# A hybrid attention and convolution layer: the norm weights spread by TensorE, the first loads in another order, and the last pair of heads handed to its out-projection inside the core

## The chip, the core and the metric

The kernel runs on one core of one Trainium2 chip. A core has five engines that run side by side, each through its own instruction list, in order: PE (TensorE, matmuls and transposes; PEld is its weight load), DVE (VectorE), ACT (ScalarE), POOL (GpSimd) and SP (SyncE). SP and POOL here only issue DMAs between DRAM and the core's memory; an issue that has to wait holds up the issues behind it in the same list. The metric is the device time of one execution in microseconds. Three runs of the kernel before gave 921.63, 918.69 and 923.97 us.

## The reference, cut to what matters

```python
def reference(x, norm_g, w_in, conv_w, conv_b, conv_ln_g, conv_ln_b, w_out, final_norm_g):
    for layer in range(DEPTH):                      # one layer, x is 1024 x 1024 float32
        h = rmsnorm(x, norm_g[layer])
        proj = jnp.einsum('bsd,de->bse', h, w_in[layer])          # 1024 -> 5632 columns
        q, k, v, a_gate, c_val, c_glu, c_gate = jnp.split(proj, split_idx, axis=-1)
        y_att = attention_branch(q, k, v, a_gate)
        y_conv = conv_branch(c_val, c_glu, c_gate, conv_w[layer], conv_b[layer],
                             conv_ln_g[layer], conv_ln_b[layer])
        y = jnp.concatenate([y_att, y_conv], axis=-1)
        x = x + jnp.einsum('bse,ed->bsd', y, w_out[layer])
    return rmsnorm(x, final_norm_g)
```

`attention_branch` runs 16 query heads of 64 over 4 key heads, in three dilated causal windows (128 by step 1, 512 by 4, 2048 by 16), whose results are mixed by their softmax denominators, times `silu(a_gate)`. `conv_branch` is `val * sigmoid(glu)`, a causal depthwise convolution of 31 taps, a layer norm, `silu`, and times `silu(c_gate)`.

## The kernel before

**Numbers.** TensorE works in float32r, which keeps fewer bits than float32. So each float32 operand is split in a rounded high part and a low part (`split_r`: ACT casts the high part, DVE subtracts), and each product of two operands is three matmuls: high x high, high x low, low x high. For most blocks of w_in the low part is made otherwise (`split_dma`): ACT writes the high part and its negative, and a DMA on POOL's queue that adds on the way (`add_into`) adds the raw weights to the negative.

**Start.** `prepare(half)` loads x in blocks of 128 rows, squares and sums them on ACT, takes 1/root, multiplies by that and by the norm weights (`gbc`, the row norm_g loaded by one DMA into all 128 partitions), transposes each block on TensorE into two banks `xT`, and splits these into `hhi` and `hlo`, the stationary side of every input projection. Before that TensorE makes 45 idle transposes (`idle`) on the identity.

**Input projections.** A block of 128 columns of w_in (`raw`, split in `wh` and `wl`) times both halves of h gives two banks `ps`, 24 matmuls of 512 columns each. h0 to h7 are the GLU and value blocks of the convolution, k, v, q and a those of attention, c0 to c7 the gate of the convolution. `SECTIONS` says which blocks go beside which pair of heads.

**Attention.** `attend(p)` handles heads 2p and 2p+1: scores `sc`, on DVE table and minimum (`near`, `far`: `add_min`), exponentials `e` on ACT, transposes `tp`, sums `on` and `of` with the high and low parts of v side by side in the 128 output rows. So in `comb` the upper 64 rows have to be added to the lower 64. The kernel does it by DMA: SP stores the lower rows to the tile `y`, POOL's adding DMA adds the upper rows, DVE multiplies by the gate (`y<-y,ag`), and SP stores `y` to `y_dram`, for each of the eight pairs. At the end `att_part(tb)` loads `ya`, 128 columns of all eight pairs, splits it and multiplies by `woah` and `woal`, made by `load_wo_att` from eight loads `raw_oa`, of which two can be held at a time (`opsa`, 16 banks of 24 matmuls).

**Convolution.** `convolve(p)` runs the 31 taps on DVE. `layer_norm(half)` loads the sums again (`cc`), normalizes, gates and stores to `yc_dram`. `load_wo` makes `woc`, and `conv_part(tb)` the last product `opsc` and the final norm.

**Order.** Every operation is recorded with a price and is put in order by a planner (`Plan.order`), which plays the engines through, starting what its prices say can start first, with priority by place in the program and by `boost` (`TUNE`). `LIMITS` says how many tiles of a name may be alive. The result is one fixed order on each engine; in the run the engines wait for one another by semaphores.

Of the kernel before, what the change touches and what calls it, by code (L numbers as in the profile page):

```python
# [34 lines left out]
LIMITS = {"x": 5, "raw": 2, "raw_oc": 1, "raw_oa": 2, "wh": 2, "wl": 3, "tab": 2, "e": 7, "pt": 5, "vs": 4, "vc":  # L35
          4, "turn": 2, "score": 2, "hc": 5, "c": 7, "t": 1, "g": 1, "gl": 7, "y": 1, "ag": 4, "cc": 10, "qs": 6,
          "qf": 4, "kdh": 9, "kdl": 6, "yc": 1, "ya": 2, "zc": 8, "za": 3}
# [3 lines left out]
WARM = 45  # L41
TUNE = {"w": 125, "use": 250, "ln": 65, "att": 230, "conv": 85, "wo": 125, "woa": 100, "ap": 170, "wait": 0.2116}
SECTIONS = [("h1 v k0 q0", 0), ("h2 a0 q1", 1), ("h3 a1 q2", 1), ("h4 a2 q3", 1), ("h5 k1 a3 q4", 1),
            ("h6 a4 q5 c0", 1), ("h7 a5 q6 c1 q7", 1), ("a6 a7 c2 c3", 1), ("c4 c5", 1), ("c6 c7", 0)]
# [115 lines left out]
class Plan:  # L160
# [5 lines left out]
    def __init__(self, tc, slots, limits):  # L166
        self.tc, self.nc = tc, tc.nc
        self.slots = slots
        self.limits = limits
        self.ops = []  # L170
        self.moved = []
        self.prio, self.boost = [], 0
        self.ranks = {}
        self.tables = {}
# [11 lines left out]
    def op(self, engine, cost, fn, outs, ins):  # L186
        i = len(self.ops)
        deps, bufs = set(), set()
# [24 lines left out]
        self.prio.append(i - self.boost)  # L213
# [21 lines left out]
    def act(self, out, x, func, bias=None, scale=None, accum=None):  # L235
        nc = self.nc
        kw = {"bias": bias, "scale": scale, "accum_out": accum}
        kw = {k: v for k, v in kw.items() if v is not None}

        if func in (AF.Exp, AF.Tanh, AF.Sqrt):  # L240
            self.tables[len(self.ops)] = func is AF.Sqrt

        def fn():
            if func is AF.Copy and not kw:
                nc.scalar.copy(out.ap(), x.ap())  # L245
            else:
# [3 lines left out]
        self.op("ACT", (0.051 if near else 0.0935) + x.cols / 1200.0 + 0.0935 * ptrs, fn,  # L250
                [out] + ([accum] if accum else []), [x, bias, scale])

# [4 lines left out]
    def stt(self, out, a, s, b, op0, op1):  # L257
        self.op("DVE", 0.0685 + a.cols / 960.0 + (0.061 if isinstance(s, View) else 0.0),
# [13 lines left out]
    def add_min(self, out, a, b, first, least):  # L272
# [3 lines left out]
                [out, least], [a, b, first])  # L276

# [130 lines left out]
    def trace(self):  # L408
# [40 lines left out]
def layer_kernel(tc, x, norm_g, w_in, conv_w, conv_b, ln_g, ln_b, w_out, fin_g, tab, out):  # L449
# [30 lines left out]
    avg = fixed([P, P], "avg", avg_t, True)  # L480
    par = fixed([P, 8 * NPAR], "par", const([P, 8 * NPAR], "par"), False)
# [47 lines left out]
    idle = bank("sc", "idle")  # L529
    pl.mm([(idle[:, 0:P], ident, ident, None, None)] * WARM)  # L530
    gbc = c4([P, D], "gbc")
    rows = c4([P, D], "rows")

    first_w = {2: C_GLU, 3: C_VAL}
    raw, ready = {}, {}

    def prepare(half):
        xs = []
        for j in range(4):
# [7 lines left out]
        rs = []  # L547
        for j in (0, 2):
            st = pl.buf("st", [P, 8], F32, f"xst{half}{j}")
            ms, v, t, r = (st[:, 2 * k:2 * k + 2] for k in range(4))  # L550
            for k in range(2):
                junk = pl.buf("c2", [P, D], BF16, f"junk{half}{j + k}")
                pl.act(junk, xs[j + k], AF.Square, accum=ms[:, k:k + 1])
            pl.ts(v, ms, 1.0 / D, NORM_EPS, ALU.mult, ALU.add)
            rsqrt(r, v, t)
            rs += [r[:, 0:1], r[:, 1:2]]
        for j in range(4):
            tb = 4 * half + j
            xt, o = xs[j], j * P
# [6 lines left out]
            if tb in first_w:  # L566
                ready[first_w[tb]] = split_w(first_w[tb], raw[tb], split_r)

    def parameters():
# [3 lines left out]
        b = bank("sc", "par_ps")  # L573
# [23 lines left out]
    def load_w(col):  # L597
# [3 lines left out]
        w = split_w(col, load_raw(col))  # L601
# [153 lines left out]

    def attend(p):
# [126 lines left out]
        for r0 in (0, 2):  # L883
            whole = turned(f"w{r0}", [(at(2 * r + j), far_e(j, r0 + r, 1)[:, 0:P])
                                      for r in range(2) for j in range(2)], P)
            for r in (r0, r0 + 1):
# [11 lines left out]
                yield 1.0  # L898
        for j in range(2):
# [60 lines left out]

    wo_conv, wo_att = [], [[[None] * 8, [None] * 8] for _ in range(2)]
# [12 lines left out]
    def outproj(name, tb, y_src, z_src, w, cuts=(0, 512, 1024), after=lambda zc: None):  # L974
        y = c4([P, 8, P], f"y{name}{tb}")
# [3 lines left out]
        yh, yl = c4([P, 8, P], f"yh{name}{tb}", F32R), c4([P, 8, P], f"yl{name}{tb}", F32R)  # L979
        split_r(yh, yl, y)  # L980
        for n0, n1 in zip(cuts, cuts[1:]):
            b = bank("mm", f"ops{name}{tb}_{n0}")[:, 0:n1 - n0]
            half, cs = n0 // 512, slice(n0 % 512, n0 % 512 + n1 - n0)
            for f in range(8):
                wh, wl = w[half][0][f][:, cs], w[half][1][f][:, cs]
                pl.mm([(b, yh[:, f, :], wh, f == 0, False),
                       (b, yh[:, f, :], wl, False, False),
                       (b, yl[:, f, :], wh, False, f == 7)])
# [6 lines left out]
    def att_part(tb):  # L995
        rows = slice(tb % 2 * 512 + tb // 2, tb % 2 * 512 + 512, 4)
        z = yield from outproj("a", tb, y_dram, x[rows, :], wo_att)
        pl.store(z_dram[rows, :], z)

    def conv_part(tb):  # L1000
# [13 lines left out]
        z = yield from outproj("c", tb, yc_dram, z_dram[rows, :], wo_conv, cuts, square)  # L1014
# [90 lines left out]
```

## Time and profile before

| | us |
|---|---|
| median of three runs | 921.63 |
| lowest and highest | 918.69 and 923.97 |
| profiled execution | 918.28 |
| span of its instructions | 916.3 |
| PE busy in the span | 868.6 |

The profile is of one execution. A matmul's row gives its start and how long it takes from start to end; matmuls overlap, so that what one costs in a row of them is the distance of two starts. The square brackets behind a row hold how long the engine was idle before it and what released it. The clock in the windows' rows is the granted clock of TensorE as a share of 2.4 GHz; 0.50 is 1.2 GHz.

### The profile page before, as it was taken

The numbers are of one execution on the slowest core, as the hardware profiler recorded it, in microseconds if no ns is written. First come the engines' busy times: TensorE is split into PE (matmuls) and PEld (weight loads), VectorE is DVE, ScalarE is ACT, GpSimd is POOL, SyncE is SP. The second block draws the span as 40 slices with busy tenths as digits, with TensorE's granted clock in tenths as the row PEclk, the third lists the DMA queues.
The fourth block names the chain that finished last, engine by engine and source line by source line (L and its number), as shares of the span: only waits on it lengthen the run. The fifth ranks groups of instructions, "written<-read, shape, count | busy, mean of one in ns | idle before, by whom it ended". The sixth has DMA issues, their size and how long they took to land.

```text
span 916.3 us, 12908 instructions
## 1 busy us (share of the span) xinstructions
PE 868.6 (95%) x4449; PEld 724.4 (79%) x4449; DVE 649.6 (71%) x1490; ACT 591.8 (65%) x1392; POOL 56.5 (6%) x72
## 2 busy tenths in 40 slices
PE   6899999999999999999998999899994899999996
PEld 6888878888888888878887888788783787878886
DVE  4769985699699899589568846984576953644532
ACT  5743679778878789768956875795897623514211
POOL 0010000011000110011001101001001000000000
PEclk7999999999999999999998999999997899999999
DMA  8732317246554664436506726347969785579111
GB/s 270 196 69 68 93 32 155 47 93 148 108 121 90 132 145 95 80 81 142 137 25 161 161 51 157 71 117 157 282 224 255 245 300 193 172 237 280 64 51 46
DMA packets 106870, 127.19 MB, mean 139 GB/s; under 512 B 18068, under 2 KB 79508, under 8 KB 106806
## 3 DMA queue, kind: packets, MB, share of 16 engines
q1 hardware_dynamic: 98470, 96.49, 34.2%
q0 software_dynamic: 8336, 29.89, 18.4%
q8 instruction: 35, 0.57, 0.2%
q14 instruction: 29, 0.24, 0.1%
HBM read 66.40 MB, written 25.36 MB: 100 GB/s over the span
## 4 chain that ended last, share of the span: by engine, by line
PE 58%; DVE 16%; DMA 13%; ACT 8%; issue 3%; SPq 1%; POOL 0%; DVEq 0%; ACTq 0%; POOLq 0%
PE ps L232 34%; PE opsc L232 10%; DMA y<-comb 6%; DVE c L259 3%; DMA raw_oc<-in_w_out 3%; ACT e L247 3%; PE on L232 2%; PE of L232 2%; DVE cc L259 2%; PE sc_1near L232 2%; DVE t L259 2%; ACT pt L245 1%; DMA x<-in_x 1%; PE sc_0near L232 1%; SPq L280 1%
## 5 line engine op out<-in xcount | busy, mean ns | idle before, releaser
L232 PE MATMUL ps<-hhi,wl 128*128 128x512 f32 (+1 forms) x720 | 282.2, 392 | 14.7 <-DMA wl<-raw 14.7
L232 PE MATMUL ps<-hhi,wh 128*128 128x512 f32 (+1 forms) x720 | 290.7, 404 | 1.1 <-ACT wh L245 1.1
L232 PE MATMUL ps<-hlo,wh 128*128 128x512 f32 (+1 forms) x720 | 281.8, 391 | 0.0
L232 PEld LDWEIGHTS ps<-hhi,wl 128*128 128x128 f32 x720 | 137.1, 190 | 45.5 <-DMA wl<-raw 15.1
L232 PEld LDWEIGHTS ps<-hhi,wh 128*128 128x128 f32 x720 | 137.5, 191 | 24.9 <-ACT wh L245 2.1
L232 PEld LDWEIGHTS ps<-hlo,wh 128*128 128x128 f32 x720 | 137.6, 191 | 23.0 <-issue 0.2
L247 ACT ACTIVATE e<-e,near 128x256 f32<-128x256 f32 (+1 forms) x256 | 114.9, 486 | 19.3 <-DVE near L255 15.6
L259 DVE SCALAR_TENSOR_TENSOR c<-hc,taps,c 128x511 f32<-128x511 f32 (+14 forms) x120 | 88.6, 738 | 2.1 <-ACT c L247 1.8
L259 DVE SCALAR_TENSOR_TENSOR c<-t,taps,c 128x511 f32<-128x511 f32 (+14 forms) x120 | 88.7, 739 | 0.1
L259 DVE SCALAR_TENSOR_TENSOR t<-hc,taps,t 128x511 f32<-128x511 f32 (+6 forms) x112 | 82.9, 740 | 0.9 <-ACT t L247 0.8
L232 PE MATMUL opsc<-woc,yhc 128*128 128x512 f32 (+1 forms) x272 | 80.9, 381 | 0.7 <-ACT yhc L245 0.7
L247 ACT ACTIVATE e<-e,far 128x96 f32<-128x96 f32 (+1 forms) x128 | 53.9, 424 | 29.3 <-DVE far L274 28.3
L283 POOL DMA_DIRECT2D wl<-raw x42 | 36.5, 870 | 390.0 <-ACT wl L247 297.4
L232 PEld LDWEIGHTS opsc<-woc,yhc 128*128 128x128 f32 x272 | 50.0, 188 | 11.4 <-ACT yhc L245 1.1
L232 PE MATMUL opsa<-woah,yla 128*128 128x512 f32 x128 | 50.6, 396 | 2.3 <-DVE yla L255 2.3
L232 PE MATMUL opsc<-woc,ylc 128*128 128x512 f32 (+1 forms) x136 | 51.9, 382 | 0.5 <-DVE ylc L255 0.5
L232 PE MATMUL opsa<-woah,yha 128*128 128x512 f32 x128 | 50.5, 395 | 0.0
L232 PE MATMUL opsa<-woal,yha 128*128 128x512 f32 x128 | 50.5, 394 | 0.0
L245 ACT CAST wh<-raw 128x1024 fp32r<-128x1024 f32 x44 | 45.9, 1043 | 0.7 <-DMA raw<-in_w_in 0.6
L247 ACT ACTIVATE fjunk<-zc 128x512 bf16<-128x512 f32 (+1 forms) x17 | 10.3, 606 | 55.5 <-DVE zc L255 55.5
L247 ACT ACTIVATE e<-e,f 128x96 f32<-128x96 f32 (+1 forms) x128 | 45.0, 438 | 0.1
L247 ACT ACTIVATE wl<-raw 128x1024 fp32r<-128x1024 f32 x42 | 44.5, 1061 | 0.0
(160 smaller groups left out, 1476.5 us busy)
## 6 DMA issues: line engine op xcount, KB each, us to landing
raw<-in_w_in SPq DMA_DIRECT2D x44, 512.0 KB, 5.4
wl<-raw POOLq DMA_DIRECT2D x42, 512.0 KB, 5.0
x<-in_x SPq DMA_DIRECT2D x8, 512.0 KB, 11.0
tab<-in_tab SPq DMA_DIRECT2D x8, 512.0 KB, 3.5
c_dram<-c SPq DMA_DIRECT2D x8, 512.0 KB, 3.1
y<-comb SPq DMA_DIRECT2D x16, 256.0 KB, 3.8
y<-comb POOLq DMA_DIRECT2D x16, 256.0 KB, 4.9
y_dram<-y SPq DMA_DIRECT2D x8, 512.0 KB, 5.4
```

The source lines that it names most:

```text
L232: nc.tensor.matmul(out.ap(), a.ap(), b.ap(), start=start, stop=stop)
L245: nc.scalar.copy(out.ap(), x.ap())
L247: nc.scalar.activation(out.ap(), x.ap(), func, **{k: ap_of(v) for k, v in kw.items()})
L259: lambda: self.nc.vector.scalar_tensor_tensor(out.ap(), a.ap(), ap_of(s), b.ap(), op0, op1),
L280: self.op("SP", 0.48, lambda: self.nc.sync.dma_start(out.ap(), ap_of(src)), [out], [src, after])
L283: self.op("POOL", 1.0, lambda: self.nc.gpsimd.dma_start(ap_of(dst), x.ap(), accum_op=ALU.add), [dst], [x, dst])
```

## The change

1. The norm weights are loaded as one row (`gain`); two matmuls with a row of 1/1024 spread them over the partitions into two PSUM banks, and each block of x is multiplied in two halves of 512 columns. The factor 1/1024 is taken back in the norm's constants. The second block's squares are summed on DVE. Ten more idle transposes stand at the front and 22 between the first blocks.
2. The GLU weights of h0 are loaded ahead of the third block of x. Their low part, and that of the value weights, are made behind the first two blocks' splits. Squares of later blocks are held until a named earlier split has been made (`hold`, which only sets the plan's order).
3. The last pair of heads isn't stored: TensorE adds the halves of `comb` with a matrix of ones (`fold`, float32, into the banks `y7_0` and `y7_1`), DVE multiplies by the gate, and ACT and DVE split the result into `ylast`, which `opsa` reads from the core's memory; `ya` holds seven pairs.
4. The low parts of the last two gate blocks (c6, c7) are made by `split_r` rather than by DMA.
5. Both halves of the layer norm stand with the attention's out-projection; the planner's prices, limits, boosts and the order of blocks are other numbers.

```diff
-LIMITS = {"x": 5, "raw": 2, "raw_oc": 1, "raw_oa": 2, "wh": 2, ... "tab": 2, ... "pt": 5, ... "y": 1, ... "cc": 10, ...
+LIMITS = {"x": 5, "raw": 2, "raw_oc": 1, "raw_oa": 2, "wh": 3, ... "tab": 1, ... "pt": 4, ... "y": 2, ... "cc": 5, ...
-WARM = 45
+WARM = 55
+LATE = C_CG + 6 * P
+MORE = (10, 12)
-TUNE = {"w": 125, "use": 250, "ln": 65, "att": 230, "conv": 85, "wo": 125, "woa": 100, "ap": 170, ...}
+TUNE = {"w": 225, "use": 260, "ln": 65, "att": 240, "conv": -15, "wo": 185, "woa": 20, "ap": 0, ...}
-SECTIONS = [("h1 v k0 q0", 0), ("h2 a0 q1", 1), ...
+SECTIONS = [("k0 q0 h1 v", 0), ("h2 a0 q1", 1), ...
...
-        self.op("ACT", (0.051 if near else 0.0935) + x.cols / 1200.0 + 0.0935 * ptrs, fn,
+        slow = 2.0 if not near and x.cols > 1 and x.idx.ravel()[1] - x.idx.ravel()[0] > 1 else 1.0
+        self.op("ACT", (0.051 if near else 0.0935) + slow * x.cols / 1200.0 + 0.0935 * ptrs + self.cross(out, x), fn,
...
-                self.dma_time[i] = 4.0 * self.moved[i] / (360e3 if e == "SP" else 150e3)
+                self.dma_time[i] = 4.0 * self.moved[i] / (300e3 if e == "SP" else 175e3)
...
-    gbc = c4([P, D], "gbc")
+    gain = c4([1, D], "gain")
+    gbc = [bank("sc", f"gbc{i}") for i in range(2)]
-    first_w = {2: C_GLU, 3: C_VAL}
+    first_w = {1: C_GLU, 3: C_VAL}
...
             if tb == 1:
-                pl.load(gbc, norm_g.partition_broadcast(P))
+                pl.load(gain, norm_g.rearrange("(o d) -> o d", o=1))
...
+            for i in range(2):
+                pl.mm([(gbc[i], avg[0:1], gain[:, i * 512:i * 512 + 512], True, True)])
...
-            pl.stt(xt, xt, rs[j], gbc, ALU.mult, ALU.mult)
             for cg in range(2):
-                b = bank("tp", f"xT{half}{j}_{cg}")
+                part = xt[:, cg * 512:cg * 512 + 512]
+                pl.stt(part, part, r[:, j % 2:j % 2 + 1], gbc[cg], ALU.mult, ALU.mult)
+                b = bank("mm" if tb == 1 else "tp", f"xT{half}{j}_{cg}")
...
+            if tb < len(MORE):
+                pl.mm([(idle[:, 0:P], ident, ident, None, None)] * MORE[tb])
...
-        w = split_w(col, load_raw(col))
+        w = split_w(col, load_raw(col), split_r if col >= LATE else split_dma)
...
+        if p == NH // 2 - 1:
+            for n in range(2):
+                both = bank("tp", f"y{p}_{n}", "turn")
+                pl.mm([(both, fold[:, DH - j * DH:192 - j * DH], comb[:, j, 2 * n:2 * n + 2].flat(), j == 0, j == 1) for j in range(2)])
+                part = y[:, 2 * n:2 * n + 2].flat()
+                pl.stt(part, both, 0.5, ag[p][:, 2 * n:2 * n + 2].flat(), ALU.mult, ALU.mult)
+                split_r(y_last[0][:, 2 * n:2 * n + 2].flat(), y_last[1][:, 2 * n:2 * n + 2].flat(), part)
+            return
...
-        pl.load(z, z_src)
-        pl.load(y, y_src[:, :, tb * P:(tb + 1) * P], after=z)
+        if not last:
+            pl.load(z, z_src)
+        pl.load(y, y_src[:, 0:n, tb * P:(tb + 1) * P], after=w[1][1][7] if last else z)
...
-    section(9, 8.0, [boosted("ln", layer_norm(0))], [(8.0, [boosted("woa", load_wo_att())])])
+    section(9, 8.0, [boosted("woa", load_wo_att())])
-    together((14.0, [boosted("ln", layer_norm(1))]), (8.0, [boosted("wo", load_wo("c", D, wo_conv))]),
+    together((28.0, [boosted("ln", layer_norm(half)) for half in range(2)]), (8.0, [boosted("wo", load_wo("c", D, wo_conv))]),
```

How the instructions stand, at three places. First PE, the front of its list before (xT_0_180 and xT_1_185 are the first block of x, the next two pairs the second and third block):

```order
L230 MATMUL idle<-ident 128x128 x45
L230 MATMUL xT_0_180<-ident,x_145 128x128 x4
L230 MATMUL xT_1_185<-ident,x_145 128x128 x4
L230 MATMUL xT_0_206<-ident,x_147 128x128 x4
L230 MATMUL xT_1_216<-ident,x_147 128x128 x4
L230 MATMUL xT_0_238<-ident,x_151 128x128 x4
L230 MATMUL xT_1_244<-ident,x_151 128x128 x4
L232 MATMUL ps_0_252<-hhi_194,wh_192 128x256
```

And now, with the two matmuls that spread the norm weights:

```order
L234 MATMUL idle<-ident 128x128 x55
L236 MATMUL gbc_182<-gain,avg 128x512
L236 MATMUL gbc_185<-gain,avg 128x512
L234 MATMUL idle<-ident 128x128 x10
L234 MATMUL xT_0_206<-ident,x_158 128x128 x4
L234 MATMUL xT_1_215<-ident,x_158 128x128 x4
L234 MATMUL idle<-ident 128x128 x12
L234 MATMUL xT_0_242<-ident,x_160 128x128 x4
L234 MATMUL xT_1_248<-ident,x_160 128x128 x4
L236 MATMUL ps_0_275<-hhi_234,wh_188 128x256
```

The first projection moved ahead of the third block's transposes; the norm weights' matmuls stand ahead of the first block's.

Next POOL, the end of its list before (y_6842 is the last pair of heads, wl_6864 the low part of the weights of c7):

```order
L283 DMA y_6228<-comb_5915 64x1024 x2
L283 DMA wl_6419<-raw_6265 128x1024
L283 DMA y_6842<-comb_6533 64x1024 x2
L283 DMA wl_6864<-raw_6580 128x1024
L1101 UNCONDITIONAL_BRANCH
```

And now (y_6211 is the last but one pair, wl_6238 and wl_6250 belong to c4 and c5):

```order
L297 DMA y_6211<-comb_5881 64x1024 x2
L297 DMA wl_6238<-raw_6077 128x1024
L297 DMA wl_6250<-raw_6209 128x1024
L1155 UNCONDITIONAL_BRANCH
```

The last pair's adds are gone, and no low part stands behind them.

Last SP, around the loads of the attention's out-projection weights before:

```order
L286 DMA y_6842<-comb_6533 64x1024 x2
L286 DMA g_dram<-g_6827 128x1024
L280 DMA raw_oa_6858<-in_w_out 128x1024
L280 DMA raw_oa_6869<-in_w_out 128x1024
L280 DMA raw_oa_6890<-in_w_out 128x1024
L286 DMA y_dram<-y_6842 128x1024
L286 DMA yc_dram<-cc_0_6287 128x512
L280 DMA raw_oa_6915<-in_w_out 128x1024
L286 DMA yc_dram<-cc_0_6287 128x512
L286 DMA yc_dram<-cc_1_6336 128x512 x2
L280 DMA ya_6949<-y_dram 128x8x128
```

And now (g_6855 is the gate of c6, cc_0_6909 the layer norm's second half):

```order
L294 DMA raw_oa_6720<-in_w_out 128x1024
L294 DMA raw_oa_6722<-in_w_out 128x1024
L294 DMA gl_0_6769<-g_dram 128x2x512
L294 DMA gl_2_6800<-g_dram 128x2x512
L294 DMA gl_4_6833<-g_dram 128x2x512
L294 DMA raw_oa_6883<-in_w_out 128x1024
L300 DMA g_dram<-g_6855 128x1024
L294 DMA raw_oa_6899<-in_w_out 128x1024
L294 DMA cc_0_6909<-c_dram 128x2x512
L294 DMA raw_oa_6913<-in_w_out 128x1024
L294 DMA ya_6981<-y_dram 128x7x128
```

The last weight load no longer stands behind the store of the last pair, but three of the eight still stand in a row of single issues, each of which needs a free one of two tiles.

## Rows read from the trace of the kernel before

**Rows 1.** Windows: us, busy of each engine, PEclk, DMA share, GB/s
```profile
0.00:42.00 42.00, 31.33 (x208) 29.56 (x209) 23.88 (x48) 24.79 (x52) 1.83 (x8) 0.84 0.82 254
42.00:684.00 642.00, 630.92 (x3314) 527.38 (x3314) 500.93 (x1232) 479.69 (x1201) 52.13 (x61) 0.99 0.49 114
684.00:725.00 41.00, 25.55 (x126) 20.80 (x123) 33.98 (x54) 30.20 (x43) 2.52 (x3) 0.79 0.89 265
725.00:819.00 94.00, 91.20 (x400) 73.39 (x398) 53.32 (x84) 34.33 (x48) 0.00 (x0) 1.00 0.67 224
```

**Rows 2.** Waits of PE: us in total, times, longest
```profile
PE ps L232 <- DMA wl<-raw: 14.7, 1, 14.7
PE xT L230 <- DVE hlo L255: 7.8, 3, 3.6
...
PE sc_0far L232 <- ACT qf L245: 1.8, 3, 0.9
```

**Rows 3.** Timeline of the start: start us, us, engine, what [idle before]
```profile
1.46 7.49 PE L230 MATMUL idle<-ident 128*128 128x128 f32 x45 [1.46 <-POOL ident masks.py:199]
...
9.00 2.48 DVE L259 SCALAR_TENSOR_TENSOR x<-x,xst,gbc 128x1024 f32<-128x1024 f32 x2 [1.27 <-DMA gbc<-in_norm_g]
...
10.34 1.09 PE L230 MATMUL xT<-ident,x 128*128 128x128 f32 x8 [1.40 <-DVE x L259]
...
20.13 0.56 PE L232 MATMUL ps<-hhi,wh 128*128 128x256 f32 x1
...
23.37 1.06 ACT L247 ACTIVATE junk<-x 128x1024 bf16<-128x1024 f32 x1 [4.66 <-DMA x<-in_x]
...
25.77 1.33 PE L230 MATMUL xT<-ident,x 128*128 128x128 f32 x8 [2.73 <-DVE hlo L255]
```

**Rows 4.** A window of 2 us in the start
```profile
18.00:20.00 2.00, 1.49 (x7) 1.49 (x8) 2.00 (x3) 0.71 (x2) 0.00 (x0) 0.50 0.21 60
```

**Rows 5.** Timeline from the last pair's sums to the out-projection
```profile
692.61 0.88 PE L232 MATMUL of<-pt,vc 96*128 96x256 f32 x6
...
694.92 1.07 PE L232 MATMUL mean<-csum,avg 128*128 128x512 f32 x2
...
696.11 3.26 SPq L280 DMA_DIRECT2D raw_oa<-in_w_out  x3
...
700.54 0.90 POOL L283 DMA_DIRECT2D wl<-raw  x1
704.78 1.04 ACT L245 CAST woah<-raw_oa 128x1024 fp32r<-128x1024 f32 x1 [3.35 <-DMA raw_oa<-in_w_out]
...
709.74 1.23 DVE L259 SCALAR_TENSOR_TENSOR y<-y,ag 128x1024 f32<-128x1024 f32 x1 [2.06 <-DMA y<-comb]
...
712.17 0.80 PE L232 MATMUL ps<-hhi,wl 128*128 128x512 f32 x1 [14.68 <-DMA wl<-raw]
...
712.77 0.63 PE L232 MATMUL ps<-hhi,wh 128*128 128x512 f32 x1
```

**Rows 6.** Groups by shape on DVE: xcount, busy us, mean ns, idle before
```profile
L255 DVE TENSOR_TENSOR comb<-of,comb 128x512 f32<-128x512 f32 x32 | 22.0, 687 | 7.4 <-PE of L232 7.2
...
L255 DVE TENSOR_TENSOR woal<-raw_oa,woah 128x1024 fp32r<-128x1024 f32 x8 | 9.8, 1220 | 3.3 <-ACT woah L245 3.3
```

**Rows 7.** The tile raw_oa: its loads from issue to landing
```profile
DMA to landing us min/median/max: 3.2/6.2/9.9
```

**Rows 8.** The tile opsa: durations ns, first and last start
```profile
L232 PE MATMUL opsa<-woah,yha x128: 387/393/477, 724.7 to 817.7; 128*128 128x512 f32 x128
```

**Rows 9.** Groups by shape on ACT, two casts of 512 columns
```profile
L245 ACT CAST qf<-qs 128x512 fp32r<-128x512 f32 x32 | 34.3, 1120 | 13.0 <-DVE qs L259 12.8
...
L245 ACT CAST hhi<-xT 128x512 fp32r<-128x512 f32 x16 | 8.9, 584 | 5.1 <-PE xT L230 5.1
```

**Rows 10.** Waits of DVE for the adding DMAs
```profile
DVE y L259 <- DMA y<-comb: 10.3, 7, 2.3
```

**Rows 11.** A window of 4 us behind a wait in the middle
```profile
496.00:500.00 4.00, 3.82 (x16) 3.58 (x17) 3.92 (x15) 3.67 (x16) 0.00 (x0) 0.50 0.98 213
```

More of the change, by code (lines that the diff above doesn't have):

```diff
@@ L170, in __init__ @@
         self.ops = []
+        self.hold = []
         self.moved = []
@@ L187, in op @@
         i = len(self.ops)
+        ins, self.hold = list(ins) + self.hold, []
         deps, bufs = set(), set()
@@ L257, in stt @@
     def stt(self, out, a, s, b, op0, op1):
-        self.op("DVE", 0.0685 + a.cols / 960.0 + (0.061 if isinstance(s, View) else 0.0),
+        self.op("DVE", 0.0685 + a.cols / 960.0 + (0.061 if isinstance(s, View) else 0.0) + self.cross(out, a),
                 lambda: self.nc.vector.scalar_tensor_tensor(out.ap(), a.ap(), ap_of(s), b.ap(), op0, op1),
@@ L276, in add_min, with square_sum @@
                 [out, least], [a, b, first])
+    def square_sum(self, out, a, total):
+        self.op("DVE", 0.07 + a.cols / 960.0,
+                lambda: self.nc.vector.tensor_tensor_reduce(out.ap(), a.ap(), a.ap(), 1.0, 0.0, ALU.mult, ALU.add,
+                                                            total.ap()), [out, total], [a])
     def load(self, out, src, after=None):
@@ L543, in prepare @@
             if tb == 1:
-                pl.load(gbc, norm_g.partition_broadcast(P))
+                pl.load(gain, norm_g.rearrange("(o d) -> o d", o=1))
             if tb in first_w:
                 raw[tb] = load_raw(first_w[tb])
[L547 to L556, printed above, removed]
+        if half == 0:
+            for i in range(2):
+                pl.mm([(gbc[i], avg[0:1], gain[:, i * 512:i * 512 + 512], True, True)])
         for j in range(4):
             tb = 4 * half + j
+            if j % 2 == 0:
+                st = pl.buf("st", [P, 8], F32, f"xst{half}{j}")
+                ms, v, t, r = (st[:, 2 * k:2 * k + 2] for k in range(4))
+                for k in range(2):
+                    junk = pl.buf("c2", [P, D], BF16, f"junk{half}{j + k}")
+                    if k and j == 0 and half == 0:
+                        pl.square_sum(junk, xs[j + k], ms[:, k:k + 1])
+                    else:
+                        if half:
+                            pl.hold = [hhi[0][:, 4:8, (j + 1) * P:(j + 2) * P]]
+                        elif k:
+                            pl.hold = [hhi[0][:, 4:8, 0:P]]
+                        pl.act(junk, xs[j + k], AF.Square, accum=ms[:, k:k + 1])
+                pl.ts(v, ms, 1.0 / D / D ** 2, NORM_EPS / D ** 2, ALU.mult, ALU.add)
+                rsqrt(r, v, t)
             xt, o = xs[j], j * P
-            pl.stt(xt, xt, rs[j], gbc, ALU.mult, ALU.mult)
             for cg in range(2):
-                b = bank("tp", f"xT{half}{j}_{cg}")
+                part = xt[:, cg * 512:cg * 512 + 512]
+                pl.stt(part, part, r[:, j % 2:j % 2 + 1], gbc[cg], ALU.mult, ALU.mult)
+                b = bank("mm" if tb == 1 else "tp", f"xT{half}{j}_{cg}")
                 pl.mm([(b[:, i * P:(i + 1) * P], xt[:, (4 * cg + i) * P:(4 * cg + i + 1) * P], ident, None, None)
@@ L565, in prepare @@
                 split_r(hhi[half][:, 4 * cg:4 * cg + 4, o:o + P], hlo[half][:, 4 * cg:4 * cg + 4, o:o + P], b.split(P))
-            if tb in first_w:
-                ready[first_w[tb]] = split_w(first_w[tb], raw[tb], split_r)
+            if tb < len(MORE):
+                pl.mm([(idle[:, 0:P], ident, ident, None, None)] * MORE[tb])
+            for k in sorted(first_w) if tb == 1 else ():
+                col = first_w[k]
+                w = c4([P, ND, P], f"wh{col}", F32R), c4([P, ND, P], f"wl{col}", F32R)
+                pl.act(w[0], raw[k], AF.Copy)
+                pl.hold = [hlo[0][:, 0:4, P:2 * P]]
+                pl.tt(w[1], raw[k], w[0].cast(F32), ALU.subtract)
+                ready[col] = w
     def parameters():
@@ L753, in convolve @@
             pl.add_into(csum, c.flat())
+    y_last = [c4([P, 4, 256], f"ylast{k}_", F32R) for k in range(2)]
     def attend(p):
@@ L959, in load_wo @@
             yield 1.0
+    pl.tt(fold[:, DH:P], ident[:, 0:DH], ident[:, DH:P], ALU.add)
     wo_conv, wo_att = [], [[[None] * 8, [None] * 8] for _ in range(2)]
@@ L972, in load_wo_att, with outproj @@
             yield 1.0
-    def outproj(name, tb, y_src, z_src, w, cuts=(0, 512, 1024), after=lambda zc: None):
-        y = c4([P, 8, P], f"y{name}{tb}")
+    def outproj(name, tb, y_src, z_src, w, last=(), cuts=(0, 512, 1024), after=lambda zc: None):
+        n = 8 - len(last)
+        y = c4([P, n, P], f"y{name}{tb}")
         z = c4([P, D], f"z{name}{tb}")
-        pl.load(z, z_src)
-        pl.load(y, y_src[:, :, tb * P:(tb + 1) * P], after=z)
-        yh, yl = c4([P, 8, P], f"yh{name}{tb}", F32R), c4([P, 8, P], f"yl{name}{tb}", F32R)
+        if not last:
+            pl.load(z, z_src)
+        pl.load(y, y_src[:, 0:n, tb * P:(tb + 1) * P], after=w[1][1][7] if last else z)
+        yh, yl = c4([P, n, P], f"yh{name}{tb}", F32R), c4([P, n, P], f"yl{name}{tb}", F32R)
         split_r(yh, yl, y)
+        if last:
+            pl.load(z, z_src, after=yl)
+        rows = [(yh[:, f, :], yl[:, f, :]) for f in range(n)] + list(last)
         for n0, n1 in zip(cuts, cuts[1:]):
-            b = bank("mm", f"ops{name}{tb}_{n0}")[:, 0:n1 - n0]
+            b = bank("mm", f"ops{name}{tb}_{n0}", "opsa" if name == "a" else None)[:, 0:n1 - n0]
             half, cs = n0 // 512, slice(n0 % 512, n0 % 512 + n1 - n0)
@@ L996, in att_part @@
         rows = slice(tb % 2 * 512 + tb // 2, tb % 2 * 512 + 512, 4)
-        z = yield from outproj("a", tb, y_dram, x[rows, :], wo_att)
+        z = yield from outproj("a", tb, y_dram, x[rows, :], wo_att,
+                                [tuple(v[:, tb // 2, tb % 2 * P:tb % 2 * P + P] for v in y_last)])
         pl.store(z_dram[rows, :], z)
@@ L1013, in conv_part @@
         rows = slice((tb % 4) * 256 + tb // 4, (tb % 4) * 256 + 256, 2)
-        z = yield from outproj("c", tb, yc_dram, z_dram[rows, :], wo_conv, cuts, square)
+        z = yield from outproj("c", tb, yc_dram, z_dram[rows, :], wo_conv, (), cuts, square)
         st = pl.buf("st", [P, 8], F32, f"fst{tb}")
```

28 lines of the change are left out of this document (17 added, 11 removed).

## The prediction

> **What bounds the kernel.** I read the windows by stage first [rows 1]. The reader is to see that TensorE is the engine without slack: busy 630.9 of 642 us in the projections and attention, 91.2 of 94 in the out-projection of attention, and clearly idle in two places only, 10.7 of 42 us at the start and 15.4 of 41 us between the last attention and the out-projection. DVE has 500.9 of 642 us, so it delays TensorE by order, not by amount. Then the waits of PE [rows 2]: one wait of 14.7 us for the low part of one block's weights is nearly the whole second hole, and the transposes of x wait 7.8 us at the start. The timelines [rows 3, 5] tell what ends these waits, and the clock column what a hole costs behind it. So a change pays here only if it closes holes; all else is matmuls, whose number stays the same but for a few.
>
> The sum is made against the profiled execution, 918.28 us (span 916.3 and 2.0 around it). The median of the runs shown, 921.63, is 0.36% above it, and the result is scaled by that at the end.
>
> **The start.** Removed is the 512 KB load of the norm weights, for which the first product waited until 9.00 [rows 3]. In its place stands a chain on PE: 55 idle transposes instead of 45. 45 took 7.49 us, and late ones, as the transposes at 10.34 show, take 0.11 (8 in 1.09), so 55 end at 1.46 + 7.49 + 1.1 = 10.05. Behind them stand two float32 matmuls of 512 columns. The nearest row is the mean, one such matmul with 128 rows in two records, 1.07 us [rows 5]; one row deep it may be the same or, from below, an ordinary 0.24 (384 matmuls of the out-projection in 93 us [rows 8]). I take 0.9, since the columns are the same. The first product then starts at 11.0, two microseconds later than before. This edit alone is a loss.
>
> The other order of instructions gives it back. Before, PE's list had the third block's transposes ahead of the first projection, which began at 20.13, and after 12 short matmuls PE stood again, until 25.77, for the next block's transposes: they waited for a split, the split for ACT, and ACT for a load of x that landed at 23.37 [rows 3]. Now the first projection follows the second block. Its path: products of two blocks, four halves of 0.64, 11.0 to 13.8; the last transposes about 15.9, behind 22 more idle ones at 0.11; ACT's and DVE's splits of four banks at 0.58 and 0.69 [rows 6, 9], and two low parts of weights at 1.22 [rows 6], to about 19.4. So it starts a little earlier, but 30 short matmuls of 256 columns (0.12, half of 0.24) stand ahead of the fourth block's first transposes rather than 12, and I put PE there at about 24.5. That is 1.3 us earlier with 18 x 0.12 = 2.1 more work done, and some of the half-clock stretch behind it (0.50, which is 1.2 GHz, at 18 to 20 [rows 4]) falls away: minus 4. Bounds: minus 6.5, if the 7.8 us of these waits nearly vanish, and plus 2, the later first product with nothing gained.
>
> In the window 18 to 20 the DMA engines moved 60 GB/s at a share of 0.21 [rows 4] while ACT still waited for a load of x issued long before. The Trainium skill ("DMA: Bandwidth & Descriptors", section "Why a DMA increments its semaphore by 16 and not by 1") says that a plain load is spread over as many DMA engines as divide its outer size, so that one with an odd number of partitions can fall on a single engine. The trace agrees with an uneven load: a mean share of 0.21 is about three busy engines of 16. By that rule the 31 rows of the convolution's weights, which keep their place ahead of this load of x, would hold it up as before, and the term would be about minus 2 rather than minus 4; my range has both.
>
> **The handover.** Removed: the wait of 14.68 us for the weights of c7. Their adding DMA was issued at 700.54, behind the last pair's two adds on POOL's list, and landed at about 712; now no POOL DMA stands there and DVE makes the low part. The half clock behind the wait (durations of 0.63 instead of 0.39 [rows 5, 8], until about 716) goes with it, some 2 us. The last pair's way through memory goes too.
>
> What is late next is the weights of the out-projection. Count from the end of the last sums, 693.5 [rows 5]. Before, the first `opsa` came at 724.7 [rows 8], 31.2 us later. Now PE has from there 9 + 48 projection matmuls at 0.23 (13.2), the second half of the fold, two float32 matmuls (1.8), and the layer norm's three small groups (2.3): ready after 17.3. But three of eight weight tiles are still to be loaded, two may be alive, and the issues stand singly on SP's list. The first goes when DVE has done the last sum, a gate, a split (0.69 each) and a low part (1.22), at 3.5 with the hops. It lands after L; a cast (1.04), the split of the folded pair on ACT and DVE (0.6 and 0.69, ahead in both lists) and a low part (1.22) follow, 3.8 with hops; then the last tile's load L again, cast and low part 2.3, three DVE operations of 0.69 ahead in its list, the norm's short chain with two of 0.69 (2.4), and the split of `ya` (1.1), with 0.8 of hops. Sum: 3.7 + L + 3.8 + L + 2.3 + 2.1 + 2.4 + 1.1 + 0.8 = 16.2 + 2L. L was 3.2 to 9.9, median 6.2 [rows 7]. The median fell in a stretch with 265 GB/s [rows 1]; the last pair's stores and adds and one weight add are now missing there, so I take 4.7, between least and median: 25.6, and with 8 us of idling the clock will fall again, 2 more: 27.6, against 31.2 which held its own loss. That is minus 3.6. Ahead of it PE has the fold's first half (plus 1.8) and six projection matmuls and one group fewer (minus 2.3): minus 4 in all. Bounds: L of 3.2, minus 7; L of 9.9, plus 6. So of 16.7 us removed about 12 come back as another wait.
>
> DVE and ACT carry more just ahead: the layer norm's first half is squeezed in the same 16 us as the last sums. By the list, 23 DVE operations of 0.69 (15.9 us) stand against as much of PE. I take 1.5 lost, between 0 and 4. On DVE two weight blocks add 2 x 1.22, on ACT 2 x 1.06 go; both lie beside PE's work, and without that cover they would cost 2.4.
>
> **The middle.** Order and prices are all new, with the same matmuls. PE idles 11.1 of these 642 us [rows 1], and the half clock at 496 to 500 [rows 11], behind a wait of 2 us, cost some 3.6: at most 14.7 can be won. The new prices touch two real misjudgements: a cast of strided columns takes 1.12 us where a contiguous one takes 0.58 [rows 9] and is now priced double (PE waited 1.8 us for it [rows 2]), and convolution work on DVE now ranks behind attention's. Against it: DVE's 10.3 us of waits for the adding DMAs [rows 10] stay in seven of eight pairs, and their price fell. I take minus 4, between minus 11 and plus 10, which is two new places like that at 490 (6.4 with its clock) less what others give.
>
> **The out-projection.** DVE had 53 of 94 us; the second part of the norm's first half adds 24 operations of 0.69, to 70. It fits, but the DMA share was 0.67 and rises by an estimated 0.1, and loads take longer. I take plus 1, from 0 to 12.
>
> **Sum.** Minus 4, minus 4, plus 1.5, minus 4, plus 1: minus 9.5, to 908.8, scaled 912. The terms that I took from the middle of wide bounds lean, in the middle above all, to the side of waits that shrink; I say 911.
>
> **Rivals.**
> - *The new wait eats it.* If the two loads in a row take 7 us each, opsa comes 30.2 us behind the last sums, 32 with the clock: the handover then gives nothing, and start and middle give 4: 918 to 922. For it: the median of 6.2, and issues one by one. Against: less traffic.
> - *The middle's waits vanish.* If the new prices fit, 11 of the 14.7 go: 911 - 7 = 904, and with L near 3.2 some 897. For it: the strided cast. Against: the DMA waits remain, and the order of each block is new.
> - *Slower: the norm in the out-projection.* Layer norm stores, `za`, `ya` and `woc` loads share SP's list, and `opsc` waits behind the norm's last stores. If DMA rises from a share of 0.67 to over 0.9, each of eight `ya` loads comes some 2.5 us late, 20 us in all: 930. It decides once a `ya` load takes over the 11 us of two banks. For it: 265 GB/s at a share of 0.89 was reached in the stretch ahead. Against: 20 us of slack on DVE and a two tile prefetch.
>
> **Numbers.** Forecast 0.47 (905 to 917); the new wait 0.20; the middle 0.20; slower 0.13. Within 0.5%, 917 to 926, is what can't be told from no change. Faster: 0.47 x 0.95 + 0.20 + 0.20 x 0.1 = 0.67; same 0.2; slower 0.13. The range is 893 to 924, which leaves the slow case and the far end of the fast one outside.
>
> **What would show it.** Start: first product near 11 rather than 9, first projection near 19, no wait at the fourth block. Handover: no wait for `wl`, instead one of 4 to 9 us ahead of `rb` or `opsa` for DVE's chain, half clock behind it, and two loads of `raw_oa` in sequence. Middle: PE's idle time under 11 us. It is wrong if `opsa` follows the last projection without a wait, if a low part by DMA is waited for elsewhere, or if `opsa` stands for `ya`.

## The result, and the profile after

The changed kernel takes 909.52 us (median of 4 runs, 908.88 to 911.08), the kernel before, beside it, 920.16 (916.23 to 923.97): a ratio of 0.9887, 95% interval 0.9841 to 0.9934. Forecast were 911 and a range of 893 to 924. That the total came out so close is luck: two wrong terms cancel, as a division of the two profiled executions at events that both have shows:

| stretch | before | after | difference | forecast |
|---|---|---|---|---|
| start to the end of the last sums `of` | 693.5 [rows 5] | 692.4 | -1.1 | -7.0 |
| from there to the first `opsa` | 31.2 [rows 5, 8] | 20.5 | -10.7 | -3.6 |
| `opsa`, first to last start | 93.0 [rows 8] | 96.2 | +3.2 | +1 |
| profiled execution | 918.28 | 910.03 | -8.25 | -9.5 |

(The forecast of the first row is -4 for the start, +1.5 for the crowding, -4 for the middle, +1.8 for the fold's first half and -2.3 for projections that now stand behind the sums.) The windows of the changed kernel, columns as in [rows 1]:

```profile
0.00:42.00 42.00, 38.45 (x266) 34.71 (x267) 27.82 (x61) 25.74 (x54) 2.05 (x9) 0.96 0.75 229
42.00:560.00 518.00, 509.66 (x2684) 428.47 (x2683) 420.90 (x1008) 385.67 (x949) 43.55 (x51) 1.00 0.45 103
560.00:600.00 40.00, 32.57 (x152) 27.01 (x151) 35.81 (x98) 30.19 (x81) 1.75 (x2) 0.83 0.42 92
600.00:684.00 84.00, 84.00 (x461) 71.53 (x460) 44.81 (x123) 64.78 (x169) 5.99 (x7) 1.00 0.67 184
684.00:713.00 29.00, 26.71 (x130) 20.88 (x128) 25.32 (x41) 16.11 (x25) 0.00 (x0) 0.97 0.56 183
713.00:812.00 99.00, 94.59 (x404) 75.68 (x403) 65.62 (x104) 46.45 (x66) 0.00 (x0) 0.97 0.74 250
```

The two holes of [rows 1] are nearly closed: 3.6 us of idle TensorE at the start rather than 10.7, 2.3 at the handover rather than 15.4. The middle, 42 to 684, has grown a hole: 15.8 us idle (8.3 + 7.4 + 0) where 11.1 were, and a clock of 0.83 behind it. The waits of PE (us in total, times, longest) name the new ones, where [rows 2] had 14.7 for `wl` and 7.8 for `hlo`:

```profile
PE ps L236 <- DMA wl<-raw: 4.8, 4, 4.1
PE sc_1far L236 <- DVE far L283: 4.5, 1, 4.5
PE opsa L236 <- DVE yla L264: 2.6, 2, 2.2
```

The start in the timeline (start us, us, engine, what, idle before), against [rows 3]:

```profile
9.26 1.98 PE L236 MATMUL gbc<-gain,avg 1*128 1x512 f32 x4
10.41 2.92 DVE L268 SCALAR_TENSOR_TENSOR x<-x,xst,gbc 128x512 f32<-128x512 f32 x4 [2.06 <-PE gbc L236]
15.77 0.39 PE L236 MATMUL ps<-hhi,wh 128*128 128x256 f32 x1 [0.24 <-ACT hhi L249]
18.23 0.38 PE L236 MATMUL ps<-hhi,wl 128*128 128x256 f32 x1 [1.35 <-DVE wl L264]
21.24 1.06 ACT L251 ACTIVATE junk<-x 128x1024 bf16<-128x1024 f32 x1 [2.95 <-DMA x<-in_x]
24.10 0.66 PE L234 MATMUL xT<-ident,x 128*128 128x128 f32 x4
```

The first product is 1.4 us later than before, the fourth block's transposes come at 24.10 without a wait. ACT still waits 2.95 us for a load of x; no wait of TensorE follows from it.

The handover, against [rows 5]:

```profile
689.97 0.34 SPq L294 DMA_DIRECT2D raw_oa<-in_w_out  x1
...
691.09 1.28 PE L236 MATMUL of<-pt,vc 96*128 96x256 f32 x6
...
697.11 0.38 SPq L294 DMA_DIRECT2D raw_oa<-in_w_out  x1
698.41 0.47 SPq L294 DMA_DIRECT2D raw_oa<-in_w_out  x1
...
698.91 1.21 DVE L264 TENSOR_TENSOR woal<-raw_oa,woah 128x1024 fp32r<-128x1024 f32 x1
...
703.20 1.05 ACT L249 CAST woah<-raw_oa 128x1024 fp32r<-128x1024 f32 x1
704.57 1.05 ACT L249 CAST woah<-raw_oa 128x1024 fp32r<-128x1024 f32 x1 [0.32 <-DMA raw_oa<-in_w_out]
...
707.28 0.69 DVE L264 TENSOR_TENSOR woc<-raw_oc,woc 128x512 fp32r<-128x512 f32 x1 [0.40 <-PE ps L236]
...
711.29 1.92 PE L236 MATMUL rb<-ident,lst 128*128 128x128 f32 x8 [2.29 <-DVE lst L268]
712.87 0.77 PE L236 MATMUL opsa<-woah,yha 128*128 128x512 f32 x1
```

The sixth of the eight weight loads went out at 689.97, before the last sums. Only two are open behind them, and these run beside each other: issued 1.3 us apart, cast 1.4 us apart. The eighth goes out at 698.41, before the low part of the sixth is made (698.91), so three tiles are held for a while where the program's limit says two.

And the tiles `raw_oa` and `opsa`, against [rows 7, 8]: the loads are a little faster, the out-projection a little slower.

```profile
DMA to landing us min/median/max: 3.7/5.1/6.1
```

```profile
L236 PE MATMUL opsa<-woah,yha x112: 387/393/774, 712.9 to 808.4; 128*128 128x512 f32 x112
...
L236 PE MATMUL opsa<-woah,ylast__6867 x16: 392/392/398, 718.7 to 809.1; 128*128 128x512 f32 x16
```

### The profile page after: what moved, and what is told of

Read it like the earlier page. It is cut to its first block, busy times and chain, and to the rows that moved or that the text cites. A ratio compares the mean times of both kernels' runs of the same rounds, so it can differ in the third digit from the quotient of the medians.

```text
span 908.2 us, 13036 instructions
## 1 busy us (share of the span) xinstructions
PE 875.1 (96%) x4493; PEld 731.2 (81%) x4493; DVE 656.1 (72%) x1506; ACT 591.3 (65%) x1392; POOL 53.3 (6%) x69
## 5 line engine op out<-in xcount | busy, mean ns | idle before, releaser
L236 PEld LDWEIGHTS opsc<-woc,yhc 128*128 128x128 f32 x272 | 50.1, 188 | 10.7
L236 PE MATMUL opsa<-woah,yla 128*128 128x512 f32 x112 | 45.0, 402 | 2.6 <-DVE yla L264 2.6
L236 PE MATMUL opsa<-woah,yha 128*128 128x512 f32 x112 | 45.6, 408 | 0.4 <-DVE cc L264 0.4
L236 PE MATMUL opsa<-woal,yha 128*128 128x512 f32 x112 | 45.1, 402 | 0.0
L251 ACT ACTIVATE e<-e,f 128x224 f32<-128x224 f32 (+1 forms) x128 | 45.0, 436 | 0.0
L249 ACT CAST qf<-qs 128x512 fp32r<-128x512 f32 x32 | 34.3, 1120 | 13.5 <-DVE qs L268 13.5
```

Of the source, the lines that this page charges most:

```text
L236: nc.tensor.matmul(out.ap(), a.ap(), b.ap(), start=start, stop=stop)
```

## The experiments

Every time is a median; every ratio is to runs of the kernel before on the same chip.

| kernel | us | ratio, 95% interval |
|---|---|---|
| changed | 909.52 | 0.9887, 0.9841 to 0.9934 |
| `fold_off` | 916.27 | 0.9973, 0.9954 to 0.9993 |
| `late_off` | 908.04 | 0.9888, 0.9858 to 0.9918 |
| `both_off` | 922.79 | 1.0043, 1.0023 to 1.0062 |
| `start_old` | 911.35 | 0.9924, 0.9899 to 0.9950 |
| `more0` | 910.47 | 0.9909, 0.9877 to 0.9942 |
| `old_numbers` | 942.79 | 1.0249, 1.0206 to 1.0293 |
| `new_numbers` | 935.23 | 1.0172, 1.0130 to 1.0214 |
| `dve_2176` | 907.02 | 0.9862, 0.9817 to 0.9907 |
| `scores_first` | 910.03 | 0.9901, 0.9870 to 0.9932 |
| `reserve5` | 891.95 | 0.9687, 0.9654 to 0.9721 |
| `late_off_dve_reserve5` | 893.47 | 0.9710, 0.9676 to 0.9743 |
| `before_reserve5` | 932.09 | 1.0109, 1.0069 to 1.0150 |

An edit also makes the planner write a new order; only `scores_first` keeps the order of the changed kernel but for the moved instructions.

**What closed the hole at the handover.** Three kernels without one or both of its edits.

```diff
 fold_off:
-        if p == NH // 2 - 1:
+        if p == NH // 2:
...
-        z = yield from outproj("a", tb, y_dram, x[rows, :], wo_att,
-                                [tuple(v[...] for v in y_last)])
+        z = yield from outproj("a", tb, y_dram, x[rows, :], wo_att)
 late_off:
-LATE = C_CG + 6 * P
+LATE = C_CG + 8 * P
 both_off: both
```

> Leaves out one part of the change: the last pair of heads goes through memory again (two adding DMAs, gate, store, and an eighth row in each load of ya), the rest stands. Theory A (the last pair's way through memory is late): in the kernel before, its gate stood on DVE 15.5 us behind the last sum; with a store, a load and a split behind that, opsa comes some 25 us behind the last sum, against 20.5 measured in the changed kernel; TensorE gets back 3.7 us of float32 matmuls, 1.9 of them ahead of the last sum. Sum plus 3 to plus 6: 912 to 916. Theory B (the weights of the out-projection set the end, the fold only costs TensorE's time): minus 3, 906.

> Leaves out one part of the change: the low parts of the last two convolution gate blocks are made by adding DMAs again; the last pair is still folded by TensorE. Theory A (the wait of 14.7 us came from the last pair's two adds ahead on POOL's list, and the fold alone takes these away): within 2 us of 909.5, rather below it, as DVE has 2.4 us less to do in the handover. Theory B (an adding DMA in this stretch of full DMA engines lands 9 us behind its issue, as one at 483 us in the changed kernel does): a wait of 4 us or more for wl is back, 914 to 920.

> Leaves out both: last pair through memory and low parts of the last two blocks by adding DMAs; start, order numbers and layer norm as in the changed kernel. By the prediction's sum the handover was worth 4 us: 913.5. By the trace of the changed kernel (20.5 us from the last sum to opsa instead of 31.2, with 1.9 of fold ahead of it) it is worth 9 to 12: 918 to 921.

Without both, 13.3 us are lost, not the 4 of the prediction. Each edit alone closes a part: the fold 14.8 (922.8 to 908.0), the low parts on DVE 6.5 (922.8 to 916.3). Together they give 13.3, so beside the fold the low parts on DVE give nothing; the 1.5 us between `late_off` and the changed kernel don't show in the ratios. From 42 to 684 us TensorE idles 15.6 to 16.8 us in all four, so these differences don't come from the middle. The waits of `both_off` from 690 to 740 us, and its POOL list there:

```profile
PE rb L236 <- DVE lst L268: 9.6, 1, 9.6
PE opsa L236 <- ACT yha L249: 8.5, 1, 8.5
```

```profile
681.64 0.86 POOL L297 DMA_DIRECT2D wl<-raw  x1 [23.59 <-PE mean L236]
697.81 0.82 POOL L297 DMA_DIRECT2D y<-comb  x1 [15.31 <-ACT sq L251]
```

No wait for `wl` is left here although it is made by an adding DMA: the new order issues it 16 us ahead of the last pair's adds, where before it stood behind them (700.54 in [rows 5]). So the wait that [rows 2] showed was taken away by the new order, without either edit; what the edits shorten is the way of the last pair and DVE's chain, which that wait had covered. With the low parts on DVE and the pair through memory (`fold_off`) these two waits are 5.7 and 4.0; in the changed kernel the first is 2.3 and the second is gone.

**The start.**

```diff
 start_old: idle transposes, norm weights and prepare() of the kernel before (WARM = 45)
 more0:
-MORE = (10, 12)
+MORE = (0, 0)
```

> Only the start as before (norm weights by one 512 KB load to all partitions, 45 idle transposes, old order of the first instructions); all else as changed. The prediction put the start at 4 us: 913.5. The trace of the changed kernel, in which TensorE stands 1.7 us between 11 and 42 us rather than 7.8 and shows full clock from 9 us on, says 5 to 6: 915. If it were worth nothing (the later first product eats the rest): 909.5.

> The changed kernel without the 22 idle transposes behind the first two blocks of x. They take 2.4 us of TensorE. Theory A (TensorE waits for splits there anyway): nothing gained, and the clock, full from 9 us on in the changed kernel, falls to half in 12 to 20 us: plus 1 to plus 3, 910.5 to 912.5. Theory B (they stand on the path to the first projection): minus 1 to minus 2, 907.5 to 908.5.

Neither can be told from the changed kernel (1.8 and 1.0 us slower, overlapping intervals). The theory of 5 to 6 us for the new instructions fell. Without the 22 idle transposes the clock does fall at 12 to 16 us, as theory A had it; first `more0`, then the changed kernel:

```profile
12.00:16.00 4.00, 3.65 (x16) 2.90 (x14) 3.68 (x7) 2.56 (x5) 0.00 (x0) 0.57 1.04 379
```

```profile
12.00:16.00 4.00, 3.76 (x34) 3.48 (x32) 3.04 (x7) 2.99 (x6) 0.00 (x0) 1.00 1.03 378
```

No loss clear of the noise follows from it. The changed kernel isn't at full clock from 9 us on, as both expectations say: behind waits of 1.35 us and less at 16 to 18 us it stands at 0.57 from 18 to 22 us, `more0` there at 0.64. The next pair of runs tells where the start's gain comes from.

**Order numbers and code apart.**

```diff
 old_numbers: changed code, LIMITS, TUNE and SECTIONS of before (but the limit of 2 for opsa stays)
 new_numbers: code of before, LIMITS, TUNE and SECTIONS of the change
```

> The changed code, but with the limits, priorities and sections of the kernel before (only the limit for opsa, which that one lacks, is kept at 2). It tells what the new numbers are worth by themselves. By the prediction's terms the middle's new order is worth 4 and the out-projection costs 1: 912 to 914. Theory B (the numbers belong to the code: with the old ones the layer norm and the weights of both out-projections stand in the wrong places of the new order, holes of over 10 us ahead of the first opsa and the first opsc): 925 to 940. At the start the old sections bring back the old order behind the second block of x.

> The other half of the comparison: the code of the kernel before with the new limits, priorities and sections, nothing else of the change. Theory A (the start's gain is the order's, not that of the new instructions): the waits of the transposes of x at the start are gone here too, 4 to 6 us, and the hole at about 569 us is here as well, 8 us; at the handover the weights and the last pair still come late, 15 us or more ahead of the first opsa: 922 to 932. Theory B (the start's gain comes from TensorE spreading the norm weights): the waits of 7.8 us stay, 926 to 938.

Each half alone makes the kernel slower, by 2.5% and 1.7%; only together they are faster. In `old_numbers` the holes are where theory B had them:

```profile
PE opsc L236 <- ACT yhc L249: 11.1, 1, 11.1
PE opsa L236 <- ACT yha L249: 10.9, 1, 10.9
```

and in `new_numbers` at the start, as its theory B had it, and ahead of two `opsa`:

```profile
PE opsa L232 <- DVE yla L255: 12.5, 1, 12.5
PE opsa L232 <- ACT yha L245: 9.2, 1, 9.2
PE xT L230 <- DVE hlo L255: 8.1, 3, 3.4
```

How many projection matmuls (tile `ps`, in parentheses) are started in the first 60 us, in five kernels: before, `new_numbers`, `old_numbers`, `start_old`, changed.

```profile
0.00:60.00 60.00, 33.56 (x172) 0.89 0.67 195
```

```profile
0.00:60.00 60.00, 33.47 (x173) 0.89 0.73 204
```

```profile
0.00:60.00 60.00, 32.72 (x163) 0.91 0.66 187
```

```profile
0.00:60.00 60.00, 38.16 (x188) 0.94 0.74 204
```

```profile
0.00:60.00 60.00, 38.63 (x192) 0.97 0.66 191
```

The new numbers alone bring nothing, the new code with old numbers less than nothing. `start_old`, which has the new numbers and the planner's new prices but the old first instructions, has 16 of the 20 matmuls gained. So, by elimination, the planner's new prices and the numbers together moved the first projection forward; the new first instructions go with the last 4. No run has the prices alone.

**The two new waits of the middle.** First the one at 492 us, by DVE in place of an adding DMA for that one block:

```diff
-split_r if col >= LATE else split_dma
+split_r if col >= LATE or col == C_AG + 640 else split_dma
```

> The changed kernel with the low part of one more weight block (the sixth of the attention gate's, waited for 4.1 us at 492 us) made by DVE instead of an adding DMA. Theory A (the adding DMA landed 9 us after its issue because two weight loads were issued within 0.3 us of it; made on the spot from the loaded tile it is there at once): minus 4.1 and minus 1.8 of half clock: 903 to 905. Theory B (the block's load itself is late, since loads and adds share the same full DMA engines): a wait of 2 to 4 us for the cast or the low part stays, 907 to 910.

The wait between 470 and 500 us fell from 4.1 to 1.3 us, for another block's adding DMA. The median is 2.5 us lower, under half of what theory A gave, and the intervals overlap: the wait is shown, its price is not.

Then the one at 569 us. In the changed kernel, TensorE stands because the reductions of its scores stand behind a gate and query splits on DVE:

```profile
564.06 1.23 DVE L268 SCALAR_TENSOR_TENSOR y<-y,ag 128x1024 f32<-128x1024 f32 x1 [0.86 <-DMA y<-comb]
...
568.19 0.26 DVE L283 CUSTOM_DVE_ANT_0 e<-sc_1far,tab 128x96 f32<-128x96 f32 x1
...
568.71 1.05 ACT L249 CAST wh<-raw 128x1024 fp32r<-128x1024 f32 x1
...
569.14 0.56 PE L236 MATMUL sc_1far<-kdh,qf 128*128 128x224 f32 x1 [4.49 <-DVE far L283]
```

```diff
 scores_first, on the finished order:
+ gate y5 and its store, two steps of c7, splits and casts of two query blocks
+ go behind the first three reductions of sc6_1far
```

> The changed kernel with its order frozen, and at one place (569 us) eight instructions moved: the gate y of the sixth pair with its store, two convolution steps, and the splits and casts of two query blocks now stand behind the first three reductions of the far scores of the seventh pair, which they stood ahead of on DVE. Theory A (TensorE's wait of 4.5 us there and the half clock behind it come from these 4 us of DVE work ahead in the list, so the change's new order lost them): the wait shrinks to about 1 and takes a part of the half clock with it, 901 to 905. Theory B (with two score banks and the first of them held until 575 us, DVE is the bound of this whole stretch and the work only comes later): within 2 us of 909.5.

Theory B came true, with no gain: 0.81 us is left of the wait, and the next scores wait 5.36 us instead.

```profile
572.66 0.48 PE L237 MATMUL sc_0near<-kdh,qs 128*128 128x128 f32 x1 [5.36 <-DVE far L284]
```

But theory B says that DVE is the bound, and that is not the end of it. In the changed kernel's timeline no projection stands between the scores at 563 and 578.5: the next block's weights had been requested at 538 and were cast only at 568.71. By the planner's count, 25 of 33 tiles were in use then and 8 kept free for scores and their transposes. So one number was changed that the change had not touched:

```diff
-RESERVE = {"e": 7, "pt": 3}
+RESERVE = {"e": 5, "pt": 3}
```

> The changed kernel with one number less: of the 33 tiles of 4 KB, the planner keeps 5 free for the scores (e) rather than 7. Theory A (the hole at 569 us is not DVE's: TensorE had no projection left to put between the scores, because the next block's weights, loaded since about 543 us, found no tile for their split until 568.7; 25 tiles were in use and 8 kept free): the split comes earlier, the hole and its half clock go, minus 7 to minus 10: 900 to 903. Theory B (DVE and ACT, 0.9 and 0.75 busy there, are the bound of that stage): the waits move to the next scores as they did when the reductions were put first, 907 to 910.

891.95 us, 17.6 less than the changed kernel, twice what theory A gave. The cast of these weights now stands at 545.52, and projections lie between the scores; of the waits from 540 to 600 us 0.3 us is left. The windows:

```profile
545.52 1.04 ACT L249 CAST wh<-raw 128x1024 fp32r<-128x1024 f32 x1
```

```profile
42.00:684.00 642.00, 636.98 (x3387) 536.97 (x3386) 519.21 (x1256) 492.06 (x1218) 51.20 (x60) 1.00 0.49 117
560.00:600.00 40.00, 39.66 (x222) 33.69 (x221) 36.21 (x109) 35.95 (x100) 2.56 (x3) 1.00 0.41 94
```

TensorE idles 5.0 us from 42 to 684 rather than 15.8, and DVE is as busy at 560 to 600 as it was (36.2 and 35.8): it was not the bound. Divided at the events of the first table, the two profiled executions differ by -14.1 us up to the end of the last sums, -4.8 from there to the first `opsa` and +1.9 in the out-projection. So the hole at 569 us is a part of the gain only; the clock, now 1.00 in the middle, has another. That the free tile did it is seen for this one block, whose cast came 23 us earlier; the number changed the whole order, and for the other waits that went it is argued. A third run adds the other two edits, a fourth gives the kernel before the same number:

```diff
 late_off_dve_reserve5: the edits of late_off, dve_2176 and reserve5 together
 before_reserve5: RESERVE as in reserve5, in the kernel before
```

> Three edits together on the changed kernel: low parts of the last two blocks by adding DMAs again (1.5 us faster by itself), low part of the one block that was waited for at 492 us by DVE (2.5 us faster by itself), 5 rather than 7 tiles kept for scores. If they add up and the third is worth 8: 897. If the order of the handover that the last edit gives costs it again, 901 to 904.

> The kernel before with 5 rather than 7 tiles kept free for scores, nothing of the change. Theory A (the gain of 17.6 us that this number gave the changed kernel is the new order's: its new waits at 180 to 270, 400, 492, 569 and 775 us came from too few free tiles): the old order, whose only wait over 1.5 us in the middle is one of 2, gains 0 to 4, 915 to 919. Theory B (the kept tiles held up weights under any order): 10 or more, 903 to 909.

The three edits don't add up: 893.47 is no better than `reserve5`, the fastest kernel here. And the kernel before becomes slower by 1.1%, which neither theory had. Its longest waits:

```profile
PE opsa L232 <- ACT yha L245: 9.4, 1, 9.4
...
PE sc_1near L232 <- DVE near L274: 5.6, 2, 3.8
PE rb L232 <- DVE lst L259: 5.0, 1, 5.0
```

The handover keeps 14 us of waits, as `opsa` and `rb` instead of `wl`, and a new wait for scores appears. Why the same number opens that one is not settled.

## Why the prediction was right in sum and wrong in two terms

*Start, -4.* The steps came as told but sooner: products at 10.41 (11.0 forecast), fourth block at 24.10 without a wait (24.5). The low part at 18.23 ended the last wait ahead of the projections, 19.4 forecast. 20 projection matmuls more are through by 60 us, between 2.4 us (0.12 each) and 4.6 (0.23), so the size fits. The mechanism was half right: the order gives it, but, by elimination, that order came from prices and numbers. That the norm weights' chain alone is no gain is borne out: `start_old` loses at most a little. The alternative of -2, from a load of x held up by the rows of the convolution's weights, went by a wait of TensorE that did not come. ACT waited 2.95 us for that load instead of 4.66, with the rows issued at 6.6 instead of 10.4; the Trainium skill's rule ("DMA: Bandwidth & Descriptors", "Why a DMA increments its semaphore by 16 and not by 1") is neither shown nor refuted here.

*Handover, -4.* Right: no wait for `wl`, one ahead of `rb` for DVE's chain (2.3 us, 4 to 9 forecast), half clock behind. Wrong: "then the last tile's load L again". The chain was put at 16.2 + 2L = 25.6 and with the clock 27.6; measured are 20.5. (Its first step is 3.5 in the prediction's text and 3.7 in its sum.) The first of the three loads had gone out 2.4 us ahead of the end of the last sums, rather than 3.7 behind it, and the other two ran side by side. The limit of two tiles is kept in the planner's time; by the code, a load on the chip waits only for the last reader of the tile that it was given. So one L had to go, and the weights left the chain by a little: their last low part was made by 706.9, then DVE stood 0.40 us for the last projection, and from there three operations and the norm's chain lead to `rb` at 711.29. That 16.2 and the measured median of 5.1 make 21.3, close to 20.5, is therefore partly luck. The gain in this stretch was 10.7, not 3.6. And the reason given for the old wait was right for the old order only: `both_off` has no such wait.

*Crowding, +1.5.* No loss shows: TensorE is busy for all of 600 to 684 us, and on to the end of the last sums.

*Middle, -4.* The sign was wrong. The prediction weighed the new prices for and against, and looked for late adding DMAs; one came, 4.1 us at 492. The larger hole, 7.4 us with half clock behind it, came from tiles kept free while weights waited for one, which the prediction did not have among its steps. It could have been read from the order: it lists the sixth pair's gate and the scores of the seventh with no projection of the next block between them.

*Out-projection, +1.* Measured 3.2. The waits for the split of `ya` are hardly longer, 2.6 us in all; in the kernel before they were

```profile
PE opsa L232 <- DVE yla L255: 2.3, 2, 1.9
```

New is half clock, in a stretch that had 1.00 [rows 1]: at 713 to 715 us behind the wait for `rb`, and behind the longer of the two waits:

```profile
775.25 0.50 PE L236 MATMUL opsa<-woah,yla 128*128 128x512 f32 x1 [2.18 <-DVE yla L264]
```

```profile
773.00:783.00 10.00, 7.82 (x28) 6.19 (x28) 9.33 (x15) 8.89 (x13) 0.00 (x0) 0.83 0.93 318
```

This `ya` had been cast at 759.1; its low part stood on DVE behind the layer norm's operations, which run without a gap from 771.1. So a part of the slow rival is there, the norm in this stretch, but not its late loads of `ya`.

*Rivals.* "The new wait eats it" needed two loads of 7 us in a row; there were two side by side, the later of which landed 6.1 us after its issue. "The middle's waits vanish" is what `reserve5` made true, and its 892 lies a little below the range's low end, since the handover had gained more than was allowed for.

## What to carry to other kernels

Where a planner writes the order, a change in code and a change of its numbers can't be judged apart: the two halves here were 2.5% and 1.7% slower alone, and one number gave 1.9% to the new order and took 1.1% from the old. When TensorE stands for a reduction on DVE, ask first why nothing else was there to run: moving the reductions forward moved the wait, giving the next weights a tile took it away. Before summing loads in a row, look which event each load waits for in the trace; a limit in the program is not a limit on the chip.

## What the runs showed of the hardware

The issue of a load can hold SP's queue far longer than its size says. In the changed kernel the 4 KB row of the convolution's bias took 7.88 us to issue, and before, loads of x took 4.96 and 7.04 there; most take 0.3 to 0.9:

```profile
10.58 7.88 SPq L294 DMA_DIRECT2D rows<-in_conv_b  x1
```

The DMA engines were busy then (a share of 0.86 at 14 to 18 us in the changed kernel); what held the issue is not shown. Whatever stands behind on that queue is late by as much, so the order of issues at a full start counts even for small loads.
